# Encoder layer in float32: a second plain half in the up projection, h's sums behind the first one, T4 of w_down's first chunk summed in DRAM, and two quarters of hT changing places

## The chip, the cores and the metric

The kernel runs on one core of a Trainium2 chip. The metric is the device time of one execution in microseconds. Engines are named as in the profile: PE multiplies matrices (PEld loads its weights), DVE and ACT work on vectors, POOL issues the transfers that add or that go from DRAM to DRAM, SP issues most of the plain loads and stores.

## The reference

One layer of an encoder over 512 tokens of 2048 channels, all in float32. Only its second half is touched by the change:

```
x  = x + rms_norm(concat(a, p) @ w_o)                     # a: attention, p: pooling
h  = rms_norm(x)                                          # (512, 2048)
up = causal_dwconv(h @ w_up)                              # w_up (2048, 11264), 3 taps along the tokens
y  = (gelu(up[..., :5632]) * up[..., 5632:]) @ w_down     # w_down (5632, 2048)
x  = x + rms_norm(y)
```

## The kernel before

**Numbers.** Every float32 operand of a product is split in two: `split` (L136) rounds it on ACT (L140, the high part) and takes the rest on DVE (L141, the low part). A product is then made of two or three passes of PE: high by high, high by low, low by high.

**Products of seven.** Large products are cut in 2 x 2 x 2 blocks, and seven products of sums of blocks are made where a plain multiplication has eight. The sums are numbered 1 to 7. Their names in the profile are the banks that hold them: `qa` (products 1, 6, 7, 4, one upon the other), `qg` (5, then 3) and `qd` (2).

**The up projection** has 44 halves: for each u of 22, one half of gates and one of the factors that they multiply, each 256 channels wide, over 512 tokens and a contraction of 2048. Before the change the first half is plain: 16 blocks of the contraction by 2 by 3 passes, 96 matmuls of 512 columns, named `up` in the profile (`mm3`, L162, L164, L165). Its weights come as four quarters `w_0` to `w_3`. The other 43 halves (k from 0 to 42) are made by seven products, each of 8 wide matmuls (512 columns, L170) and 8 narrow ones (256 columns, L176). The product of each (k, i) stands in `Factors.order`, which `seven` follows: product i of half k has the due number 7k plus its place, so that the products of neighbouring halves alternate. The products (0..3, 1) and (0..3, 2), which need only the first 256 tokens of h, are put ahead, then come four entries `("w", q)` for the plain half, then (0,5) and (0,3), and from there (0,6), (0,7), (1,5), (0,4), (1,3), (1,6), (1,7), (2,5), (1,4), (2,3), (2,6), (2,7), and so on.

**The left side** is h turned (tokens along the free axis): `hT`, four tiles of 16 KB per partition, two for each half of the contraction, each holding both halves of the tokens in high and low parts. The last 256 tokens are turned by `turn` (PE, line 1012) among the last early products and in the first two quarters of the plain half, then split into hT. Products 5, 6 and 3 need sums of the blocks of h: `h_sums` (L1374) makes them with 8 additions on DVE, and splits their results into the tiles `h5`, `h6`, `h3`. It also overwrites two quarters of hT (its first contraction half, last tokens) with the difference that product 7 needs, which must wait until the plain half has read them.

**The weights of the seven products** are sums too, and are made in place: a tile is loaded (SP), split, then the next block is added onto it by an accumulating DMA (POOL, L1108), split again. So product 6's weights follow product 5's by one such round, 4 follows 6, and 7 follows 3. `Factors.prefetch` keeps the splits four products ahead of PE. After a bank is done, ACT copies it out (`m`, L1415, L1420, L1424) before the next product may go upon it; each pair of halves ends in a gate (three taps, gelu) or a product with a gate on ACT and DVE, and is stored to DRAM (`gd`, L1346).

**Who sets the order.** PE's instructions run as written. For the other engines a scheduler orders the instructions when the program is built; each engine then runs its own in that order, so one that waits holds up those behind it.

**The down projection** runs over five chunks of w_down, by seven products for each of two column blocks cc, 24 matmuls each (banks `pa`, `pg`, `pd`). The sums of the first chunk are made ahead of time, T5, T7 and T6 in DRAM by `sums_in_dram` (its steps are taken one by one by `more_sums`, in the attention's and the output projection's time), three of the products ready split (`rw`, loaded by POOL at L1212). T4 is T6 loaded, with one more block added onto it in SBUF by an accumulating DMA when it is there (L1241). The tiles of this stage (pool `p4`) lie where hT and the weights of the up projection lay: the four buffers of `part` (copies of product banks) in the quarter at the lowest address, the fifth `part` and the first `bh` (`wh`, first filled with `rw02h`) in the next one. Before the change the lowest quarter holds hT[1] and the next one hT[2]. Products 7 read hT[0] and hT[1]; products 2 and 4 read hT[2] and hT[3], and the last products of the up projection are 7, 2 and 4 of its last half, in this order.

## Time and profile before

| | |
|---|---|
| median of 3 runs | 1881.85 us (1880.81 to 1882.25) |
| the profiled execution | 1881.14 us, its span 1879.3 us |
| PE busy | 1846.3 us, 98% of the span |
| DVE, ACT, POOL busy | 1488.1, 1104.6, 310.4 us |
| DMA | 428.11 MB; 37.7% (SP's queue) and 47.3% (POOL's queue) of the 16 engines' span |
| first plain half on PE | 573.4 to 599.2 us |
| seven products of the up projection, from there | 599.2 to 1434.2 us |
| first chunk of the down projection | 1434.2 to about 1510 us |

Times in the rows are microseconds from the span's start. A row of the timeline gives start, duration, engine, line, operation, tile written and tiles read, and in brackets how long the engine sat idle before it and who released it. A row of the waits gives the instruction that waited, whom for, the sum, how often, and the longest. A row of the windows gives a stretch, its length, each engine's busy time with its instructions, then PE's granted clock (1.00 is full), the DMA engines' busy share and GB/s.

### The profile page before, as it was taken

The page shows a single profiled execution, that of the slowest core. Times are in us where ns is not written, and L with a number is a line of the kernel's source. Part 1 is how long each engine was busy: PE and PEld are TensorE (multiplying, and loading weights), DVE is VectorE, ACT ScalarE, POOL GpSimd, SP SyncE. Part 2 cuts the span into 40 slices and gives each one's busy share as a digit, 9 for nine tenths or more (in the row PEclk, how much of TensorE's full clock was granted, in tenths as well). Part 3 has the DMA queues.
Part 4 walks back from the last instruction along what each step waited for, and adds up shares of the span by engine and source line. Part 5 has one row for each costly group of instructions (what it writes and reads, how often), then busy time and mean ns, then how long its engine had stood idle before and what let it go on. Part 6 is the DMA issues. An engine that isn't in the chain of part 4 may idle for free.

```text
span 1879.3 us, 25378 instructions
## 1 busy us (share of the span) xinstructions
PE 1846.3 (98%) x9530; PEld 1582.3 (84%) x9530; DVE 1488.1 (79%) x1782; ACT 1104.6 (59%) x1449; POOL 310.4 (17%) x411
## 2 busy tenths in 40 slices
PE   9999999999998899999999999999999989999998
PEld 7888888888886788888888888888887878888886
DVE  6988778788678678777787777877776699899876
ACT  7655455466586556665666656666564565565553
POOL 3411001100001221212222121221221101111101
PEclk9999999999999999999999999999999999999999
DMA  8699987999976888888889889888887967877785
GB/s 317 180 315 298 322 233 220 279 279 304 343 261 184 189 187 199 208 207 199 199 202 209 206 196 205 200 204 205 200 179 286 331 239 174 213 202 174 177 240 148
DMA packets 139402, 428.11 MB, mean 228 GB/s; under 512 B 12016, under 2 KB 15472, under 8 KB 133616
## 3 DMA queue, kind: packets, MB, share of 16 engines
q0 software_dynamic: 56016, 177.75, 47.3%
q1 hardware_dynamic: 83264, 248.74, 37.7%
q8 instruction: 75, 1.23, 0.3%
q14 instruction: 47, 0.39, 0.1%
HBM read 372.45 MB, written 100.14 MB: 251 GB/s over the span
## 4 chain that ended last, share of the span: by engine, by line
PE 62%; DMA 3%; DVE 3%; issue 2%; ACT 1%; POOL 0%; POOLq 0%; DVEq 0%; ACTq 0%; SPq 0%
PE qa L170 16%; PE qa L176 8%; PE qg L170 8%; PE qg L176 4%; PE qd L170 4%; PE pa L162 3%; PE pa L164 3%; PE pa L165 3%; PE qd L176 2%; PE pg L162 2%; PE pg L164 2%; PE pg L165 2%; DMA t<-in_w_down 1%; PE pd L164 1%; PE pd L165 1%
## 5 line engine op out<-in xcount | busy, mean ns | idle before, releaser
L170 PE MATMUL qa<-gT,wfh 128*128 128x512 f32 x1200 | 302.0, 394 | 0.0
L141 DVE TENSOR_TENSOR wfl<-x,wfh 128x1024 fp32r<-128x1024 f32 x165 | 202.0, 1224 | 89.4 <-ACT wfh L140 83.5
L170 PEld LDWEIGHTS qa<-gT,wfh 128*128 128x128 f32 x1200 | 216.9, 190 | 38.9
L140 ACT ACTIVATE wfh<-x 128x1024 fp32r<-128x1024 f32 x165 | 174.4, 1057 | 94.7 <-PE qg L170 48.6
L1108 POOL DMA_DIRECT2D x<-in_w_up x125 | 107.2, 858 | 494.0 <-DVE wfl L141 458.6
L170 PE MATMUL qg<-h,wfh 128*128 128x512 f32 x688 | 172.2, 392 | 7.9 <-DVE h L141 6.9
L176 PE MATMUL qa<-gT,wfl 128*128 128x256 f32 x1200 | 169.1, 284 | 5.6 <-ACT m L1420 5.6
L176 PEld LDWEIGHTS qa<-gT,wfl 128*128 128x128 f32 x1200 | 158.6, 192 | 11.1 <-ACT m L1420 6.8
L170 PEld LDWEIGHTS qg<-h,wfh 128*128 128x128 f32 x688 | 129.8, 189 | 36.3 <-DVE h L141 7.5
L140 ACT ACTIVATE bh<-b 128x2048 fp32r<-128x2048 f32 x56 | 106.1, 1914 | 69.8 <-DVE b L1222 26.8
L140 ACT ACTIVATE wfh<-wy 128x1024 fp32r<-128x1024 f32 x100 | 105.3, 1054 | 69.2 <-PE qd L170 50.9
L141 DVE TENSOR_TENSOR bl<-b,bh 128x2048 fp32r<-128x2048 f32 x56 | 127.0, 2285 | 18.8 <-ACT bh L140 11.7
L141 DVE TENSOR_TENSOR wfl<-wy,wfh 128x1024 fp32r<-128x1024 f32 x100 | 121.8, 1218 | 12.7 <-ACT wfh L140 9.6
L162 PE MATMUL pa<-bh,ah 128*128 128x512 f32 x320 | 125.7, 393 | 4.8 <-ACT part L1271 4.8
L164 PE MATMUL pa<-bl,ah 128*128 128x512 f32 x320 | 125.5, 392 | 0.0
L165 PE MATMUL pa<-bh,al 128*128 128x512 f32 x320 | 125.2, 391 | 0.0
L176 PEld LDWEIGHTS qg<-h,wfl 128*128 128x128 f32 x688 | 93.9, 190 | 6.8
L170 PE MATMUL qd<-gT,wfh 128*128 128x512 f32 x400 | 99.0, 390 | 0.0
L176 PE MATMUL qg<-h,wfl 128*128 128x256 f32 x688 | 96.0, 282 | 0.0
L170 PEld LDWEIGHTS qd<-gT,wfh 128*128 128x128 f32 x400 | 74.8, 188 | 15.3
L170 PE MATMUL qa<-h,wfh 128*128 128x512 f32 x344 | 86.2, 392 | 0.0
L141 DVE TENSOR_TENSOR wfl<-wz,wfh 128x1024 fp32r<-128x1024 f32 x50 | 61.2, 1224 | 30.9 <-PE qa L170 28.1
(569 smaller groups left out, 4266.8 us busy)
## 6 DMA issues: line engine op xcount, KB each, us to landing
x<-in_w_up POOLq DMA_DIRECT2D x125, 512.0 KB, 6.1
b<-in_w_down SPq DMA_DIRECT2D x32, 1024.0 KB, 6.9
wt<-in_w_o POOLq DMA_DIRECT2D x24, 1024.0 KB, 15.7
wz<-in_w_up SPq DMA_DIRECT2D x43, 512.0 KB, 5.6
x<-in_w_up SPq DMA_DIRECT2D x43, 512.0 KB, 5.1
wy<-in_w_up SPq DMA_DIRECT2D x43, 512.0 KB, 4.1
wy<-in_w_up POOLq DMA_DIRECT2D x43, 512.0 KB, 6.3
sum<-part POOLq DMA_DIRECT2D x38, 512.0 KB, 7.5
```

The lines of the kernel that those rows point to most:

```text
L140: rounded = nc.scalar.activation(hi, src, AF.Copy)
L141: rest = nc.vector.tensor_sub(lo, src, f32(hi))
L162: nc.tensor.matmul(ps, l[0], r[0], start=first, stop=False, skip_group_check=onto)
L164: nc.tensor.matmul(low, l[0], r[1], start=False, stop=False, skip_group_check=onto)
L165: nc.tensor.matmul(ps, l[1], r[0], start=False, stop=last, skip_group_check=onto)
L170: nc.tensor.matmul(ps, w[0][:, kb], pairs[kb][0], start=fresh and not kb, stop=last, skip_group_check=not fresh)
L176: nc.tensor.matmul(ps[:, sl], w[1][:, kb], pair[:, sl], start=False, stop=last, skip_group_check=not fresh)
L1108: nc.gpsimd.dma_start(self.raw[k, what], self.block(k, m, kh), accum_op=ALU.add)
```

## The change

The second half (the one that u = 0's gate is multiplied with) becomes plain too: `PLAIN` is 2, and the seven products make 42 halves where they made 43. The plain halves are now made by `plain(p, behind)`: behind the quarters of the first one the last tokens are turned, as before; `h_sums` is called after it; behind the quarters of the second one run the four steps of `sums_in_dram` that now make T4 (two copies of T6, two additions), and, after the first two, the splits that overwrite hT's quarters. The gate of u = 0 and its product follow the halves that they belong to. `first_right` loads T4 like any other sum, and its accumulating DMA is gone. hT[1] and hT[2] exchange their buffers, so that hT[2] now lies in the lowest quarter and hT[1] in the one that the fifth `part` and the first `bh` take later.

```diff
--- before.py
+++ after.py
@@ -28,7 +28,7 @@
 EPS = 1e-6
 WARM = 9
 NU = KF // 2
-PLAIN = 1
+PLAIN = 2
 CU = 4
 AHEAD = 3
 SCALE = 1.0 / math.sqrt(DH)
@@ -293,7 +293,7 @@
 
 
 
-    first_sum = {i: [dram.tile([P, CU, S], F32, name=f"t{i}{cc}") for cc in range(2)] for i in (5, 7, 6)}
+    first_sum = {i: [dram.tile([P, CU, S], F32, name=f"t{i}{cc}") for cc in range(2)] for i in (5, 7, 6, 4)}
 
     def sums_in_dram():
 
@@ -327,7 +327,7 @@
                             (copy, 7, (1, 1)), (add, 7, (0, 1)), (copy, 4, 6), (add, 4, (1, 0))):
             yield from wo_step(step, i, at)
         for step, i, at in ((copy, 5, (0, 0)), (add, 5, (0, 1)), (copy, 7, (1, 1)), (copy, 6, 5),
-                            (add, 7, (0, 1)), (add, 6, (1, 1))):
+                            (add, 7, (0, 1)), (add, 6, (1, 1)), (copy, 4, 6), (add, 4, (1, 0))):
             for cc in range(2):
                 step(first_sum[i][cc], first_block(cc, *at) if type(at) is tuple else first_sum[at][cc])
                 yield
@@ -1029,6 +1029,7 @@
         for t in range(2):
             load_x(t, acc8(f"x{t}", "B"))
         hT = new_gT()
+        hT[1], hT[2] = hT[2], hT[1]
         x2(0, y11, 0, whole)
         x2(0, y12, 1, whole)
         keep_x(0)
@@ -1077,7 +1078,7 @@
                        (n - 1, 7), (n - 1, 2), (n - 1, 4)]
                 order = sorted((7 * k + at, k, i) for k in range(n) for i, at in place_of.items())
                 self.order = begin + [(k, i) for _, k, i in order if (k, i) not in begin + end] + end
-                self.order[8:8] = [("w", q) for q in range(4)]
+                self.order[8:8] = [("w", q) for q in range(4 * PLAIN)]
                 self.raw, self.made, self.loaded, self.used = {}, [], 0, 0
 
             def block(self, k, m, kh):
@@ -1234,11 +1235,9 @@
     def first_right(cc, i, ring):
 
         v = ring(f"t{i}")
-        source = first_sum[6 if i == 4 else i][cc] if i in (4, *first_sum) else first_block(cc, *{2: (1, 0), 3: (1, 1)}[i])
+        source = first_sum[i][cc] if i in first_sum else first_block(cc, *{2: (1, 0), 3: (1, 1)}[i])
         with tc.issue_after(first_right.last) if first_right.last else nullcontext():
             first_right.last = nc.sync.dma_start(v, source).ins
-        if i == 4:
-            nc.gpsimd.dma_start(v, first_block(cc, 1, 0), accum_op=ALU.add)
         return v
 
     first_right.last = first_right.part = None
@@ -1386,9 +1385,8 @@
             for a11, a21, a12, a22 in halves:
                 nc.vector.scalar_tensor_tensor(a12, a22, -1.0, a12, op0=ALU.mult, op1=ALU.subtract)
             for i in range(2):
-                split(*quarter(0, 1, i), halves[i][1])
-            for i in range(2):
                 keep(3, i, (3, 2)[i], halves[i][2])
+            return [v[1] for v in halves]
 
         banks, gates = {}, {}
 
@@ -1471,20 +1469,34 @@
         start(3, 2)
         turn(2, 3)
         factors.open = True
-        ups = [bank(f"up0_{j}") for j in range(2)]
-        for q in range(4):
-            factors.used += 1
-            factors.prefetch(0)
-            factors.prefetch((2, 2, 3, factors.AHEAD)[q])
-            w = weights.get(f"w00_{q}", 0)
-            for kb in range(4 * q, 4 * q + 4):
-                for j in range(2):
-                    mm3(ups[j], part(w, j, slice(kb % 4 * P, (kb % 4 + 1) * P)), g_both(hT, kb),
-                        kb == 0, kb == KD - 1)
+        def plain(p, behind):
+            ups = [bank(f"up{p}_{j}") for j in range(2)]
+            for q in range(4):
+                factors.used += 1
+                factors.prefetch(0)
+                factors.prefetch(factors.AHEAD if p else (2, 2, 3, factors.AHEAD)[q])
+                w = weights.get(f"w{p}0_{q}", 0)
+                for kb in range(4 * q, 4 * q + 4):
+                    for j in range(2):
+                        mm3(ups[j], part(w, j, slice(kb % 4 * P, (kb % 4 + 1) * P)), g_both(hT, kb),
+                            kb == 0, kb == KD - 1)
+                behind(q)
+            return ups
+
+        def turn_two(q):
             if q < 2:
                 turn(4 + 2 * q, 5 + 2 * q)
-        h_sums()
+
+        def keep_a21(q):
+            more_sums(1)
+            if q < 2:
+                split(*quarter(0, 1, q), a21_11[q])
+
+        ups = plain(0, turn_two)
+        a21_11 = h_sums()
         gates[0] = gate(0, plain_z(ups))
+        ups = plain(1, keep_a21)
+        product(0, gates.pop(0), plain_z(ups))
         rights, firsts = [right(0, cc) for cc in range(2)], []
         for r in rights:
             next(r)
@@ -1494,7 +1506,7 @@
             r = rights[cc].send(i)
             firsts.append((firsts[0][0] if firsts else first_left(), r))
 
-        for k, i in factors.order[12:]:
+        for k, i in factors.order[8 + 4 * PLAIN:]:
             seven(k, i)
             keep(k, i)
             if (k, i) == (end, 6):
```

How the change moves instructions is shown at three places, in rows of the built programs. The first is DVE at the end of h's sums. In these rows `h` are the tiles that the products 5, 6 and 3 read, `a` the blocks of h that are summed, `wfl` the low part of weights of the seven products, `w_3l` that of a plain half's last quarter, `zc` the taps of the gate. Before, from the last third of the sums on:

```order
L141 TENSOR_TENSOR h_5661<-a_5255,h_5661 128x4x256
L141 TENSOR_TENSOR wfl<-wy,wfh 128x1024
L1384 SCALAR_TENSOR_TENSOR a_5255<-a_5255,a_4847 128x1024
L141 TENSOR_TENSOR gT_4821<-a_5254,gT_4821 128x4x256
L1387 SCALAR_TENSOR_TENSOR a_5001<-a_5255,a_5001 128x1024
L141 TENSOR_TENSOR h_5666<-a_5255,h_5666 128x4x256
L1311 SCALAR_TENSOR_TENSOR zc<-zc,vec 128x511
L141 TENSOR_TENSOR h_5678<-a_5001,h_5678 128x4x256
L141 TENSOR_TENSOR h_5675<-a_5001,h_5675 128x4x256
L1312 SCALAR_TENSOR_TENSOR zc<-zc,vec 128x510
L1311 SCALAR_TENSOR_TENSOR zc<-zc,vec 128x511
L141 TENSOR_TENSOR wfl<-x_5493,wfh 128x1024
```

And in the changed kernel:

```order
L141 TENSOR_TENSOR w_3l<-w_3r,w_3h 128x1024
L1386 SCALAR_TENSOR_TENSOR a_5003<-a_5257,a_5003 128x1024
L141 TENSOR_TENSOR h_5669<-a_5257,h_5669 128x4x256
L1310 SCALAR_TENSOR_TENSOR zc<-zc,vec 128x511 x2
L141 TENSOR_TENSOR h_5674<-a_5003,h_5674 128x4x256
L1311 SCALAR_TENSOR_TENSOR zc<-zc,vec 128x510 x2
L141 TENSOR_TENSOR wfl<-wx,wfh 128x1024
L141 TENSOR_TENSOR gT_4822<-a_5256,gT_4822 128x4x256
L141 TENSOR_TENSOR wfl<-wy,wfh 128x1024
L141 TENSOR_TENSOR gT_4824<-a_5256,gT_4824 128x4x256
L141 TENSOR_TENSOR h_5677<-a_5003,h_5677 128x4x256
```

Before, PE's product (0,5) stands directly behind the plain half, and the last h tile, which product (0,3) needs, stands behind a split of weights, two additions, a hT split and a tap. Now the weights between the sums are those of the second plain half, the last sums are followed by two hT splits that stand behind its first two quarters, and the 96 matmuls of the second plain half stand between the first one and (0,5).

The second place is SP's queue after the last quarter of the first plain half's weights (`w_3r`). `x`, `wy`, `wz` are weights of the seven products, `t` the sums of w_down in DRAM. Before:

```order
L152 DMA w_3r<-in_w_up 128x2x512
L1088 DMA x_5493<-in_w_up 128x1024
L1088 DMA wy<-in_w_up 128x1024 x2
L1088 DMA x_5493<-in_w_up 128x1024
L1088 DMA wy<-in_w_up 128x1024 x2
L1088 DMA wz<-in_w_up 128x1024
L1088 DMA x_5783<-in_w_up 128x1024 x2
L1088 DMA wy<-in_w_up 128x1024
L1088 DMA wz<-in_w_up 128x1024
```

And in the changed kernel:

```order
L152 DMA w_3r<-in_w_up 128x2x512
L1089 DMA x_5619<-in_w_up 128x1024
L152 DMA w_0r<-in_w_up 128x2x512
L152 DMA w_1r<-in_w_up 128x2x512
L1089 DMA x_5619<-in_w_up 128x1024
L152 DMA w_2r<-in_w_up 128x2x512
L152 DMA w_3r<-in_w_up 128x2x512
L312 DMA t_114<-t_112 16x16384
L312 DMA t_115<-t_113 16x16384
L1089 DMA wy<-in_w_up 128x1024 x4
L1089 DMA x_5923<-in_w_up 128x1024 x2
L1089 DMA wz<-in_w_up 128x1024
L1089 DMA wy<-in_w_up 128x1024
```

The second half's four quarters now stand where the first `wy` loads stood, and the two copies T6 to T4 stand ahead of the `wy` loads. On POOL the two additions that finish T4 stand behind the first two additions onto `x`, ahead of the first one onto `wx`:

```order
L1109 DMA x_5619<-in_w_up 128x1024 x2
L316 DMA t_114<-in_w_down 512x1x512
L316 DMA t_115<-in_w_down 512x1x512
L1109 DMA wx<-in_w_up 128x1024
L1109 DMA wy<-in_w_up 128x1024
L1109 DMA wx<-in_w_up 128x1024
L1109 DMA x_5923<-in_w_up 128x1024
L1109 DMA x_5619<-in_w_up 128x1024
L1345 DMA gd_0_5258<-zc 128x2x256
```

The third place is POOL in the first chunk of the down projection. Before, `rw` being the ready products, `sum` the stores of results, `t` the additions that made T4:

```order
L1212 DMA bh<-rw02h 128x2048
L1212 DMA bl<-rw02l 128x2048
L1596 DMA gd_5267<-ca 128x1024
L1300 DMA sum_5268<-part 128x2x512 x2
L1241 DMA t_13315<-in_w_down 128x4x512
L1241 DMA t_13353<-in_w_down 128x4x512
L1300 DMA sum_5269<-part 128x2x512 x2
L1300 DMA sum_5271<-part 128x2x512 x2
```

And in the changed kernel:

```order
L1213 DMA bh<-rw02h 128x2048
L1213 DMA bl<-rw02l 128x2048
L1608 DMA gd_5269<-ca 128x1024
L1299 DMA sum_5270<-part 128x2x512 x2
L1299 DMA sum_5271<-part 128x2x512 x2
L1299 DMA sum_5273<-part 128x2x512 x2
```

The two additions onto `t` between the stores of sums are gone; the rest keeps its order.

## The prediction

> **What bounds the kernel now.** I read first the page's busy times, then PE's waits, then the timeline around each wait, then the windows between them.
>
> ```profile
> PE 1846.3 (98%) x9530; PEld 1582.3 (84%) x9530; DVE 1488.1 (79%) x1782; ACT 1104.6 (59%) x1449; POOL 310.4 (17%) x411
> 657.16:1434.18 777.02, 777.02 (x4465) 686.30 (x4464) 603.26 (x759) 471.93 (x617) 166.05 (x200) 1.00 0.87 200
> ```
>
> PE is the bound. The second row is the long stretch of seven products: busy for all of its 777.02 us at full clock. 4464 matmuls are 279 products of 16, so a product costs 2.785 us and a half of seven 19.5 us. Nothing on another engine can shorten that stretch. What can be won lies in the waits outside it:
>
> ```profile
> PE qg L170 <- DVE h L141: 6.9, 2, 6.5
> PE qa L176 <- ACT m L1420: 5.6, 3, 4.2
> PE pa L162 <- ACT part L1271: 4.8, 1, 4.8
> PE pd L164 <- DMA bl<-rw02l: 2.4, 1, 2.4
> PE up L164 <- DVE gT L141: 1.6, 1, 1.6
> PE qg L170 <- ACT m L1415: 1.0, 1, 1.0
> ```
>
> The first, second and last row belong to the start of the seven products (599 to 657 us), the third and fourth to the first chunk of the down projection. Each long wait costs more than its length, because the clock falls to half and comes back late:
>
> ```profile
> 606.00:607.00 1.00, 0.00 (x0) 0.00 (x0) 1.00 (x3) 1.00 (x2) 0.00 (x0) 0.50 0.00 0
> 609.26 3.56 PE L170 MATMUL qg<-h,wfh 128*128 128x512 f32 x8 [6.47 <-DVE h L141]
> 613.62 1.12 PE L176 MATMUL qa<-h,wfl 128*128 128x256 f32 x8
> 652.17 2.07 PE L176 MATMUL qa<-gT,wfl 128*128 128x256 f32 x8 [4.18 <-ACT m L1420]
> 657.16 2.01 PE L170 MATMUL qg<-h,wfh 128*128 128x512 f32 x8
> 1448.06 0.50 PE L164 MATMUL pd<-bl,ah 128*128 128x512 f32 x1 [2.37 <-DMA bl<-rw02l]
> 1452.27 0.39 PE L162 MATMUL pd<-bh,ah 128*128 128x512 f32 x1
> 1508.94 0.80 PE L162 MATMUL pa<-bh,ah 128*128 128x512 f32 x1 [4.78 <-ACT part L1271]
> 1513.69 0.39 PE L165 MATMUL pa<-bh,al 128*128 128x512 f32 x1
> ```
>
> The granted clock stands seventh in a window's row (0.50 in the first). The product begun at 609.26 ends at 613.62, 4.36 us instead of 2.785: 1.6 lost. The one begun at 652.17 takes 4.99: 2.2 lost. From 1448.06 to 1452.27 there are 11 matmuls, from 1508.94 to 1513.69 another 11; 11 at full clock take 2.5 (0.227 each, by the starts of the many in a row in this stage), so 1.7 and 2.25 are lost.
>
> **The change part by part. (a) A plain half for one of seven.**
>
> ```profile
> 587.89 0.47 PE L162 MATMUL up<-gT,w_2h 128*128 128x512 f32 x1
> 593.46 0.39 PE L162 MATMUL up<-gT,w_3h 128*128 128x512 f32 x1
> 599.18 1.07 PE L170 MATMUL qg<-h,wfh 128*128 128x512 f32 x4
> ```
>
> Two quarters of the first plain half without turning behind them take 5.57 and 5.72 us, 24 matmuls each; four take 22.6. It replaces 19.5: **+3.1 us**, between 2.8 and 3.4 by the one quarter or the other. This is paid on PE in any case.
>
> **(b) h's sums behind the first half.**
>
> ```profile
> 585.62 1.22 DVE L1381 TENSOR_TENSOR a<-a,a 128x1024 f32<-128x1024 f32 x1
> 574.25 3.39 SPq L1088 DMA_DIRECT2D wy<-in_w_up  x2
> 606.20 0.74 DVE L1311 SCALAR_TENSOR_TENSOR zc<-zc,vec 128x511 f32<-128x511 f32 x1
> 606.86 2.35 DVE L141 TENSOR_TENSOR h<-a,h 128x1024 fp32r<-128x1024 f32 x2
> ```
>
> The sums begin at 585.62 and end with the two h splits at 609.2. In the changed kernel DVE has 22 instructions of this size from the first sum to the last h split, splits of weights and hT among them, and 4 taps: 22 x 1.17 + 4 x 0.74 = 28.7, from 585.62 to about 614. PE now makes 96 more matmuls from 599.2 to 621.8, (0,5) follows, and (0,3), which needs the last h, comes at 624.6: 10 us to spare. The second half's own weights ride on the same queues: SP's order puts their loads where four `wy` loads stood, the last of them issued by 577.6 (574.25 + 3.39), and their splits follow the first half's quarters, each some 15 us ahead of use. So the wait of 6.9 and the 1.6 of slow clock go: **-8.4 us** (0.40 + 6.47 + 1.57). If the cover failed altogether, 0.
>
> **(c) The start of the seven products.** The rest of the waits there are 5.6 + 1.0 and 2.2 of clock, 8.7 us. They are not h's:
>
> ```profile
> 634.95 0.86 POOL L1108 DMA_DIRECT2D wy<-in_w_up  x1 [4.76 <-DVE wfl L141]
> 640.53 1.06 ACT L140 ACTIVATE wfh<-wy 128x1024 fp32r<-128x1024 f32 x1 [3.42 <-DMA wy<-in_w_up]
> 651.54 0.58 ACT L1420 ACTIVATE m<-qa 128x512 f32<-128x512 f32 x1
> 613.44 0.86 POOL L1108 DMA_DIRECT2D x<-in_w_up  x1 [0.38 <-ACT zc L1333]
> ```
>
> For the halves 1 and 2, whose products 1 and 2 were made ahead, product 7's split stands two products (5.6 us) after product 3's, but the round between them (DVE, POOL's issue at 634.95, landing at 640.5) is longer. ACT stands at that split, and the copies that PE waits for stand behind it: PE was done at 647.99, the copy began at 651.54. The changed order keeps these rounds and moves a gate from half 1 to half 0, ahead of (1,6)'s copy; so the pattern stays, a half earlier. What gets lighter: the addition at 613.44, half 3's, falls into the second plain half and no longer stands ahead of (1,7)'s round. I take 6.0 for 8.7: **-2.7 us**, nearest to the rows; the bounds are all gone (-8.7), and as much worse as I hope for better (+2.7).
>
> **(d) hT[1] and hT[2].**
>
> ```profile
> 1433.73 0.54 POOL L1212 DMA_DIRECT2D bh<-rw02h  x1 [9.01 <-PE qa L170]
> 1434.25 0.55 POOL L1212 DMA_DIRECT2D bl<-rw02l  x1
> 1428.61 1.98 PE L170 MATMUL qd<-gT,wfh 128*128 128x512 f32 x8
> 1445.04 1.06 ACT L1271 ACTIVATE part<-pa 128x512 f32<-128x512 f32 x2
> 1455.47 1.22 DVE L141 TENSOR_TENSOR al<-s,ah 128x1024 fp32r<-128x1024 f32 x1
> ```
>
> POOL waits for the last reader of the buffer under `bh`, which is hT[2], read by the last product 4. Afterwards it is hT[1], last read by product 7, which ends where `qd` begins, 1428.61: 5 us earlier. `rw02l` landed 13.8 us after its issue; 5 earlier is 1443.0, and PE wants it at 1445.7. What comes free later, the buffers of `part`, is first written at 1445.04. So 2.37 and 1.7 go. Next in line is product (0,5), then due two products of 24 matmuls after 1445.2, at 1456.1; its left side (`al<-s`) was ready at 1456.7, and I leave 0.4: **-3.7 us**. Bounds -4.1 and 0 (if the queue brings it no sooner).
>
> The Trainium skill, TensorE: Matmul & The Clock Gate, "Part 1: The HAM clock gate", says that the clock falls to half after at least one idle window of about 3.4 us. By it the wait of 2.37 us would have cost no clock and (d) would be -2.0. The trace disagrees, since 11 matmuls after it took 4.21 us; the measurement decides.
>
> **(e) T4.**
>
> ```profile
> 1481.42 1.29 POOL L1241 DMA_DIRECT2D t<-in_w_down  x1 [1.35 <-DMA t<-t]
> 1505.54 1.91 ACT L140 ACTIVATE bh<-t 128x2048 fp32r<-128x2048 f32 x1 [8.09 <-DMA t<-in_w_down]
> 1485.07 0.51 SPq L1536 DMA_DIRECT2D gc<-gd  x1
> 1503.98 1.22 DVE L1548 TENSOR_TENSOR s<-gc 128x1024 f32<-128x1024 f32 x1 [3.60 <-DMA gc<-gd]
> ```
>
> The second addition onto T4 is issued at 1481.42 and lands at 1505.5, 24 us later. ACT stands at its split, and the copy of `part` that frees PE's bank stands behind. The changed kernel loads the finished T4, there when the addition was only issued. The `gc` load issued at 1485.07, which the same copy stands behind, took until 1504 in competition with the additions; without them I expect it some 8 us earlier, before the bank is due at about 1500. So 4.78 and 2.25 go: **-7.0 us**, at worst 0.
>
> T4's four transfers (two copies, two additions) move into the plain halves, 578 to about 612 us. That is the copies' 16.6 and the additions' 17.3 (rows below), side by side. Cover: the plain half needs none of them, and the first addition behind them has until 627.
>
> **Sum**, against the profiled execution's 1881.14: +3.1 - 8.4 - 2.7 - 3.7 - 7.0 = -18.7, 1862.4. It lies 0.7 below the median of the runs, so the forecast is **1863 us**. The wait of 1.6 for gT stays.
>
> **The rivals.**
>
> ```profile
> t<-in_w_down POOLq DMA_DIRECT2D x12, 1024.0 KB, 17.3
> wt<-wt POOLq DMA_DIRECT2D x8, 1024.0 KB, 16.6
> wx<-in_w_up POOLq DMA_DIRECT2D x3, 512.0 KB, 5.9
> ```
>
> *T4's additions hold up the weights (slower).* They stand ahead of the first `wx` addition in POOL's queue, without which (0,6), due at 599.2 + 22.6 + 2 x 2.785 = 627.4, has no weights. The copies, issued at 578, land 16.6 later, 594.6. If two additions at the worst row's 24.0 follow each other, they end at 642.6, `wx` lands at 648.5, its splits take 2.3: PE waits 23.4, loses 2.2 of clock and 3.1 more for `wy` behind it. That is 1863 + 28.7 = 1892. It decides from an end of the additions at 636 (21 us each in a row). Against it: at the median of 17.3 they end at 629 even in a row, and the one issued at 1481.42 ran beside another. By the Trainium skill (DMA: Bandwidth & Descriptors, "Queues, rings and completion order") each DMA engine takes turns between the queues but consumes one queue's descriptors in order; no run here shows this apart, and by it only POOL's own additions would be held, as assumed.
>
> *The wait at 1504 stays, with another name.* `gc` lands at 1504 as before, for it is queued behind two loads of `b` in a full DMA: the 7.0 stays, 1870. For it: it landed 19 us after its issue. Against: two accumulating megabytes are gone from that stretch.
>
> *h is late again.* ACT or DVE stands at a split of the second half's weights, and the last h comes after 624.6; some 8 us stay, 1871. Against: 10 us to spare.
>
> *The start runs clean.* With 22 us more for DMA all the 8.7 of (c) go: 1857. Against: the rounds for halves 1 and 2 begin only with their product 3, after the plain halves.
>
> *It does not do what it says*: waits move and PE merely pays the plain half, 1881 to 1884.
>
> **How the numbers follow.** Forecast (1859 to 1867) 0.57; clean start 0.10; wait at 1504 stays 0.14; h late again 0.07; no gain 0.06 (0.05 of it within 0.2%, 0.01 slower); T4's additions 0.06, of which 0.05 beyond 0.2% slower and 0.01 short of it, still faster. About 0.2%, 3.8 us, is what a measurement of this kernel tells from no change. Faster: 0.57 + 0.10 + 0.14 + 0.07 + 0.01 = 0.89; same 0.05; slower 0.06. The range goes from the clean start with (d) whole, 1856, to the wait at 1504 kept and (c) at its worse bound, 1873.
>
> **What would show it.** Right: no wait of PE on h; 96 matmuls of `up` more in 22 to 23 us; no PE wait on `rw02l` and `bh<-rw02h` issued right after product 7; no addition onto `t` near 1480 and no wait of PE on `part`; waits on `m` of about 6 us with their clock. Wrong: a wait on `wfl` at the first (0,6) would show T4 in the way; a wait on `part` released by ACT behind `gc`, the second rival; slow clock after short waits, more loss than I count.

## The result, and the profile after

The changed kernel takes 1862.2 us (median of 4 runs, 1860.06 to 1864.22) against 1881.99 (4 runs) on the same chip: a ratio of 0.9896, 95% interval 0.9879 to 0.9913. The forecast was 1863, range 1856 to 1873. The profiled execution took 1864.22, its span is 1862.4; that of before has 1879.3, so the two traces differ by 16.9 us. The sum in the prediction had said 18.7. The total is right; of its five terms, (d) did not come at all and (a) lies outside its bounds. That the forecast comes within 0.8 us of the median is in part luck: the profiled execution, in which the terms are measured below, lies 2.0 us above it.

First the page's busy times of the changed kernel:

```profile
PE 1843.5 (99%) x9514; PEld 1580.2 (85%) x9514; DVE 1482.2 (80%) x1772; ACT 1101.1 (59%) x1442; POOL 306.9 (16%) x407
```

and PE's waits (us in total, times, longest):

```profile
PE qa L176 <- ACT m L1418: 3.4, 3, 2.0
PE qg L170 <- ACT m L1413: 1.9, 3, 0.9
...
PE pd L164 <- DMA bl<-rw02l: 1.5, 1, 1.5
...
PE pd L162 <- ACT ah L140: 0.9, 1, 0.9
```

The wait on `h` (6.9) and the one on `part` (4.8) are gone. Those on `m` went from 6.6 to 5.3. The one on `rw02l` did not go: 1.5 is left of 2.4, and 0.9 on `ah` has joined it.

To see where each microsecond went, I cut the run at three instructions of PE that both kernels have: the first matmul of `up`, the first of product (0,5), the first of `pa`. The windows of before, then those of after (start and end, length, busy time of PE, PEld, DVE, ACT and POOL, PE's granted clock, DMA share, GB/s):

```profile
573.37:599.18 25.81, 24.24 (x115) 19.68 (x113) 20.98 (x20) 15.78 (x24) 3.45 (x4) 1.00 0.77 174
599.18:1434.18 835.00, 821.53 (x4689) 723.14 (x4688) 642.83 (x804) 505.07 (x660) 175.45 (x211) 0.99 0.86 198
1434.18:1870.90 436.72, 429.56 (x1885) 354.53 (x1883) 362.19 (x269) 239.61 (x251) 50.64 (x50) 0.99 0.80 221
```

```profile
572.66:619.96 47.30, 45.72 (x212) 37.78 (x210) 36.91 (x35) 28.79 (x38) 5.93 (x7) 1.00 0.93 246
619.96:1424.99 805.03, 799.74 (x4577) 704.32 (x4576) 620.40 (x778) 487.37 (x639) 172.05 (x207) 1.00 0.87 200
1424.99:1854.20 429.21, 426.81 (x1885) 353.01 (x1883) 362.29 (x269) 240.22 (x251) 47.93 (x48) 1.00 0.78 220
```

The plain halves grew by 21.49, the seven products shrank by 29.97 (19.5 of it is the half that is no longer made of seven), the down projection by 7.51. What lies before the first `up`, where the program is the same, was 0.71 shorter (in the other profiles it begins between 572.5 and 574.3, in one, plain3's, at 578.0), the tail 0.2. Together 16.9.

### The profile page after: what moved, and what is told of

It is laid out like the page before. It is cut to its first block, busy times and chain, and to the rows that moved or that the text cites. A ratio compares the mean times of both kernels' runs of the same rounds, so it can differ in the third digit from the quotient of the medians.

```text
span 1862.4 us, 25317 instructions
## 1 busy us (share of the span) xinstructions
PE 1843.5 (99%) x9514; PEld 1580.2 (85%) x9514; DVE 1482.2 (80%) x1772; ACT 1101.1 (59%) x1442; POOL 306.9 (16%) x407
## 4 chain that ended last, share of the span: by engine, by line
PE 66%; DMA 1%; DVE 1%; ACT 1%; issue 0%; POOL 0%; DVEq 0%; POOLq 0%; ACTq 0%
PE qa L170 16%; PE qa L176 8%; PE qg L170 8%; PE qg L176 4%; PE pa L165 4%; PE pa L162 4%; PE pa L164 4%; PE qd L170 4%; PE pg L165 2%; PE pg L162 2%; PE pg L164 2%; PE qd L176 2%; PE pd L164 1%; PE pd L165 1%; PE pd L162 1%; PE up L164 1%
## 5 line engine op out<-in xcount | busy, mean ns | idle before, releaser
L170 PE MATMUL qa<-gT,wfh 128*128 128x512 f32 x1176 | 295.9, 394 | 0.0
L141 DVE TENSOR_TENSOR wfl<-x,wfh 128x1024 fp32r<-128x1024 f32 x161 | 197.1, 1224 | 83.0 <-ACT wfh L140 76.8
L170 PEld LDWEIGHTS qa<-gT,wfh 128*128 128x128 f32 x1176 | 212.5, 190 | 38.2
L140 ACT ACTIVATE wfh<-x 128x1024 fp32r<-128x1024 f32 x161 | 170.1, 1056 | 88.9 <-PE qg L170 47.3
L176 PE MATMUL qa<-gT,wfl 128*128 128x256 f32 x1176 | 165.1, 283 | 3.4 <-ACT m L1418 3.4
L170 PE MATMUL qg<-h,wfh 128*128 128x512 f32 x672 | 166.4, 390 | 1.9 <-ACT m L1413 1.9
L170 PEld LDWEIGHTS qg<-h,wfh 128*128 128x128 f32 x672 | 125.8, 188 | 28.9 <-ACT m L1413 2.9
L141 DVE TENSOR_TENSOR wfl<-wy,wfh 128x1024 fp32r<-128x1024 f32 x98 | 119.4, 1218 | 16.9 <-ACT wfh L140 14.6
```

The source lines that it names most:

```text
L140: rounded = nc.scalar.activation(hi, src, AF.Copy)
L141: rest = nc.vector.tensor_sub(lo, src, f32(hi))
L170: nc.tensor.matmul(ps, w[0][:, kb], pairs[kb][0], start=fresh and not kb, stop=last, skip_group_check=not fresh)
L176: nc.tensor.matmul(ps[:, sl], w[1][:, kb], pair[:, sl], start=False, stop=last, skip_group_check=not fresh)
```

## The experiments

The medians of before on the chips of the four groups below lie between 1882.1 and 1884.4. A few us between two medians are therefore not told apart; ratios to before on the same chip, and the lengths of the three stretches in the profiles, carry the argument.

**The exchange of hT[1] and hT[2] undone (no_swap).**

```diff
-        hT[1], hT[2] = hT[2], hT[1]
```

> The changed kernel without the line that exchanges hT[1] and hT[2]. Theory A: the exchange did nothing, since the quarters' places in SBUF went along with their roles: in both kernels the quarter that product 4 reads last lies at 39936 bytes, under the buffer that rw02h is loaded into (44032), and POOL issued that load 0.45 us before the last product's end in both (1433.73 against 1434.18, 1424.54 against 1424.99). Then this kernel takes the time of the changed one, 1862.2 within 1.5, with the same two waits of PE at the second product of the down projection (0.9 and 1.5 us). Theory B: the exchange did its 3.7 us and something else gave them back; then 1866, with a wait on rw02l of 2.4 us or more.

1864.1 us, 0.9898 [0.9884, 0.9911]: the time of the changed kernel, with the same two waits at the second product, 0.92 and here 1.35 us. Theory A holds. The addresses in the built programs say why (bytes within a partition; the `bh` of rw02h lies at 44032 in all three):

```
role     before           changed          changed, without the exchange
hT[0]    gT0 at 56320     gT0 at 56320     gT0 at 56320
hT[1]    gT1 at 23552     gT2 at 23552     gT1 at 23552
hT[2]    gT2 at 39936     gT1 at 39936     gT2 at 39936
hT[3]    gT3 at 72704     gT3 at 72704     gT3 at 72704
```

The tiles changed roles, and their places changed with them. With addresses put in for names, the built programs of no_swap and of the changed kernel are the same, instruction for instruction. So hT[1] still lies in the lowest quarter after the change, and hT[2] in the one that `bh` takes, not the other way round as the section on the change has it. The changed kernel's timeline shows it at POOL's issue:

```profile
1419.42 1.98 PE L170 MATMUL qd<-gT,wfh 128*128 128x512 f32 x8
...
1424.54 0.53 POOL L1213 DMA_DIRECT2D bh<-rw02h  x1 [9.02 <-PE qa L170]
1424.99 0.39 PE L162 MATMUL pa<-bh,ah 128*128 128x512 f32 x1
...
1436.95 0.49 PE L162 MATMUL pd<-bh,ah 128*128 128x512 f32 x1 [0.92 <-ACT ah L140]
...
1438.92 0.50 PE L164 MATMUL pd<-bl,ah 128*128 128x512 f32 x1 [1.48 <-DMA bl<-rw02l]
```

`bh<-rw02h` is issued 0.45 us before `pa` begins, as it was before the change (1433.73 against 1434.18), not at `qd`, 5 us earlier.

**The exchange done in another way (wh_first).** The ring of right sides takes the place under hT[1], so the buffer comes free after product 7.

```diff
-        for r in (product_part, later["wh"], half_g, later["raw1"], ...
+        for r in (later["wh"], product_part, half_g, later["raw1"], ...
```

> The changed kernel with two rings of the last pool placed the other way round: the right sides' buffers first (23552 to 39936, under the hT quarter that product 7 reads last), the buffers of part behind them. Theory A: this is what the exchange of hT was forecast to do. POOL issues bh<-rw02h about 5.1 us earlier, just before product 7's end, rw02l lands some 5 us earlier than PE wants it, its wait of 1.48 us goes and the clock after it stays up; the wait of 0.92 on ah<-gc stays: 1.5 + 1.7 = 3.2 us less, 1859. Theory B: the landing of rw02l is set by the two transfers ahead of it and gc on the DMA engines, not by its issue: it lands no sooner, 1862. Theory C: the earlier 2 MB hold up gc, which is issued at the same moment, and PE waits for ah<-gc longer than 0.92: 1861 to 1863.

1864.47 us, 0.9902 [0.9887, 0.9916]: nothing won, though the issue moved as wanted. Its timeline:

```profile
1423.10 0.54 POOL L1213 DMA_DIRECT2D bh<-rw02h  x1 [4.36 <-PE qa L170]
...
1428.20 0.39 PE L162 MATMUL pa<-bh,ah 128*128 128x512 f32 x1
...
1441.94 0.50 PE L164 MATMUL pd<-bl,ah 128*128 128x512 f32 x1 [1.28 <-DMA bl<-rw02l]
```

and the window ahead of the landing, columns as above:

```profile
1434.00:1442.00 8.00, 5.80 (x26) 4.25 (x24) 1.22 (x1) 2.95 (x4) 0.00 (x0) 1.00 1.04 420
```

The load is issued 5.10 us before `pa`, 4.65 earlier than in the changed kernel. PE gets its data 13.74 us after the start of `pa`, where it had been 13.93: 0.2 us for 4.65. The window's row has the likely reason in its last two columns, a DMA share of 1.04 at 420 GB/s. So theory B, as far as the time goes; which transfers stood ahead is not shown. Theory C's hold-up doesn't show: the two `gc` loads of this stretch land 16.9 us after their issue (median) against 16.7 in the changed kernel.

**Two right sides made ahead instead of three (ready2).** (0,2) is then read as 1 MB raw, no longer as 2 MB ready.

```diff
-    READY = (0, 1), (1, 1), (0, 2)
+    READY = (0, 1), (1, 1)
```

> The changed kernel with two right sides of the down projection made ahead instead of three: (0,2) is no longer read as two ready parts of 1 MB each (rw02h, rw02l) but as its raw 1 MB, which ACT and DVE split then. From 1419 to 1439 us the DMA engines' busy share is 1.04 to 1.06 at 395 to 419 GB/s, and issuing rw02h and rw02l 4.7 us earlier moved the end of the wait by 0.2 us only. Theory A: what is late at the second product is set by the bytes ahead of it in that stretch, not by the issue or the buffer. One MB less is 2.5 us at 419 GB/s, ACT and DVE stand idle there (7.6 to 8.8 us) and can split: the wait of 1.48 on rw02l goes with its 1.7 us of clock, and the 0.92 on gc at least in part: 1858 to 1859. Theory B: the split, 1.9 on ACT and 2.3 on DVE, stands in the raw load's way instead, and PE waits on it about as long: 1861 to 1863.

1862.37 us, 0.9889 [0.9876, 0.9903]; not told from the changed kernel by time. The timeline tells more:

```profile
1427.38 1.92 ACT L140 ACTIVATE bh<-t 128x2048 fp32r<-128x2048 f32 x1 [2.23 <-DMA t<-in_w_down]
...
1435.05 0.50 PE L162 MATMUL pd<-bh,ah 128*128 128x512 f32 x1 [0.92 <-ACT ah L140]
...
1436.30 0.50 PE L165 MATMUL pd<-bh,al 128*128 128x512 f32 x1 [0.53 <-DVE al L141]
```

The wait on the right side is gone, its high part split by 1429.3, and the clock stays at 1.00. That agrees with theory A, but the run does not tell fewer bytes from an earlier place: the raw load is issued at 1412.1, before the DMA engines are full. The 0.92 on `ah` stays to the hundredth, which theory A had not expected, and 0.53 on `al`, made by DVE right behind `ah`, is late next. From `pa` to the end it takes 427.36 us against 429.21, as much as no_swap, where the clock happened to stay up behind both waits (427.46).

**The left sides' rings exchanged (ah_moved).** The 0.92 had the same length in ten profiles of this program and its relatives, and the releaser that ACT's row names is PE, not the load of `gc`. The built programs agree: the new `ah` lies at 109568, and since the second plain half so does `a`'s high part, which both of the first two products read. Before the change `a` lay at 121856. This kernel is ready2 and:

```diff
-        for r in (..., later["wl"], slot_h, slot_l, scratch):
+        for r in (..., later["wl"], slot_l, slot_h, scratch):
```

> As ready2, with the rings of the left sides' high and low parts exchanged in the last pool. In the changed kernel and in ready2 the wait of 0.92 on ah<-gc has been the same to the hundredth in every profile, and ACT's idle time before it ends with PE pa, not with gc: the new ah of (0,2) lies at 109568, where the high part a of the first left side lies, and PE reads that until the second product's end. Before the change a lay at 121856 and ah<-gc waited for gc alone. Theory A: this overlap makes the wait, not gc. With ah at 142336 it goes, and the low part, now at 109568, takes 0.5 to 0.7 in its place: 0.8 us less in the down projection than ready2 (426.5 from the first pa to the end, 427.36 there). Theory B: gc lands no sooner, as I had taken it before, and the wait of 0.9 on ah stays.

1862.93 us, 0.9890 [0.9873, 0.9908]: by time no difference again. By the trace it is theory A. The split's row in the changed kernel, then those of this one with PE's next wait:

```profile
1435.84 1.06 ACT L140 ACTIVATE ah<-gc 128x1024 fp32r<-128x1024 f32 x1 [8.77 <-PE pa L164]
```

```profile
1432.36 1.06 ACT L140 ACTIVATE ah<-gc 128x1024 fp32r<-128x1024 f32 x1 [0.49 <-DMA gc<-gd]
...
1436.40 1.22 DVE L141 TENSOR_TENSOR al<-gc,ah 128x1024 fp32r<-128x1024 f32 x1 [2.21 <-PE pa L164]
...
1437.68 0.50 PE L165 MATMUL pd<-bh,al 128*128 128x512 f32 x1 [0.69 <-DVE al L141]
```

ACT splits as soon as `gc` lands, and the wait on `ah` is gone. The low part, now at that address, waits for PE in its place, and PE 0.69 us for it. From `pa` to the end: 426.52, where 426.5 was expected. So the 0.92 is a wait that the second plain half brought: it moved the weights' ring on, and with it the place of `a`.

**T4 as it was (no_t4).**

```diff
+        if i == 4:
+            nc.gpsimd.dma_start(v, first_block(cc, 1, 0), accum_op=ALU.add)
...
-                            (add, 7, (0, 1)), (add, 6, (1, 1)), (copy, 4, 6), (add, 4, (1, 0))):
+                            (add, 7, (0, 1)), (add, 6, (1, 1))):
```

> The changed kernel with T4 as it was before: loaded from the finished T6 and the last block added onto it in SBUF, no sum of T4 in DRAM. Theory A: the four steps of T4 in DRAM cost nothing where they run and are worth the wait on part and its clock: 7.0 us back, 1869.2, with a PE wait of 4 to 5 us on part some 70 us into the down projection. Theory B: T4's transfers beside the plain halves cost something there, as the waits of 0.8 to 2.1 us on m: then those get shorter too, and the time is 1866 to 1868.

1873.64 us, 0.9950 [0.9936, 0.9963]; that is 9.5 more than no_swap on the same chip. The profiled execution took 1871.17, 7.0 more than the changed kernel's; it is the fastest of five. That is theory A, at 7.0 by the profile and 9.5 by the medians. In the profile all of it is in the down projection, which is as long as before the change. The start is no lighter without T4's transfers: `up` begins 1.12 us later than in the changed kernel, and the first addition onto `wx` is issued 1.11 us later, at 609.93. The windows of the seven products and of what follows:

```profile
621.08:1424.40 803.32, 798.10 (x4578) 703.08 (x4576) 620.11 (x778) 487.36 (x639) 171.60 (x207) 1.00 0.88 200
1424.40:1861.04 436.64, 427.74 (x1885) 352.86 (x1883) 362.18 (x269) 239.48 (x251) 50.57 (x50) 1.00 0.79 221
```

and PE's longest wait:

```profile
PE pa L162 <- ACT part L1272: 6.2, 2, 5.1
```

(803.32 is 1.7 under the changed kernel's 805.03. Here the clock stayed up after a wait of 2.06; there it fell. It also stayed up here behind the waits at the second product of the down projection, 0.92 and 1.58, where the changed kernel's fell. So 436.64 is better set against no_swap's 427.46, where the clock stayed up there too: 9.2, close to the 9.5 of the medians. The last section comes back to the clock.)

**T4 alone (t4_only).** The kernel before, with the sum of T4 in DRAM, its four steps behind the quarters of the single plain half. (The lines that add T4 to the sums and take its accumulating DMA away, the same as in the change, are left out here.)

```diff
...
             if q < 2:
                 turn(4 + 2 * q, 5 + 2 * q)
+            more_sums(1)
         h_sums()
```

> The kernel before with the sum of T4 in DRAM alone, its four steps behind the four quarters of the one plain half. Theory A: the sum of T4 is worth the same without the second plain half: the kernel before less 7.0, 1875, with the waits on h (6.9) and m (6.6) as they were; then the second plain half with h's sums is worth the rest, about 10 to 12. Theory B: without the second plain half the two additions of 17 us each stand ahead of the weights of product (0,6) in POOL's queue, PE waits there on wfl or m up to 10 us longer than before, and the time is 1880 or more.

1882.48 us (11 runs), 0.9989 [0.9980, 0.9998]. Alone, the sum of T4 brings next to nothing. It does what it is for. The same two windows of this kernel:

```profile
598.67:1443.12 844.45, 823.17 (x4689) 724.54 (x4688) 647.29 (x807) 507.69 (x662) 176.33 (x212) 0.99 0.87 198
1443.12:1872.37 429.25, 426.78 (x1885) 353.12 (x1883) 362.19 (x269) 240.21 (x251) 47.91 (x48) 1.00 0.79 220
```

and its timeline where the seven products begin:

```profile
581.71 1.17 POOL L316 DMA_DIRECT2D t<-in_w_down  x1 [2.28 <-DMA t<-t]
582.83 0.96 POOL L1108 DMA_DIRECT2D wx<-in_w_up  x1
...
602.19 1.06 ACT L140 ACTIVATE wfh<-wx 128x1024 fp32r<-128x1024 f32 x1 [9.52 <-DMA wx<-in_w_up]
...
609.10 2.08 PE L170 MATMUL qg<-h,wfh 128*128 128x512 f32 x4 [9.36 <-DVE h L141]
```

The down projection is 7.47 shorter than before, and the seven products are 9.45 longer. The addition onto `wx` stands right behind T4's second addition on POOL and lands 19.4 us after its issue; ACT stands 9.52 us at its split, DVE behind ACT, and `h`'s sums behind DVE. PE waits 14.2 us on `h` (9.36 and, at (0,3), 4.83) in place of 6.9. This is the prediction's first rival, with theory B's cause, at another waiter: `h`, not `wfl`. The DMA engines were full in that stretch (a share of 1.06 from 572.85 to 598.67, against 0.77 before the change), so the run doesn't tell whether POOL's order or the mere bytes held the addition up. In the changed kernel T4's additions are issued at 588.88 and 592.35 and the next `wx` addition only at 608.82, 16 us behind them.

With before, no_t4 and the changed kernel this makes a square. Lengths of the two stretches, from the profiles (us; 19.5 taken off the first where there is one plain half, as it holds one half of seven more):

```
                      T4 in SBUF                T4 in DRAM
one plain half        815.5 + 436.7 (before)    825.0 + 429.3 (t4_only)
two plain halves      803.3 + 436.6 (no_t4)     805.0 + 429.2 (changed)
```

T4 in DRAM wins 7.4 in the down projection either way as the profiles stand, and 9.2 under two halves where the clock is alike (no_t4). It costs 9.5 at the start under one plain half. Under two it costs nothing: the 1.7 between 803.3 and 805.0 is the fall of the clock.

**h's sums written behind the second half (h_late).**

```diff
...
         ups = plain(0, turn_two)
-        a21_11 = h_sums()
         gates[0] = gate(0, plain_z(ups))
-        ups = plain(1, keep_a21)
+        ups = plain(1, lambda q: more_sums(1))
+        a21_11 = h_sums()
+        for q in range(2):
+            split(*quarter(0, 1, q), a21_11[q])
```

> The changed kernel with two plain halves, but h's sums written behind the second half instead of the first. Theory A: the whole gain of the second plain half is the cover for h's sums; without it the wait for h of 6.5 to 6.9 us with 1.6 us of clock comes back, 8.4 in all: 1870.6. Theory B: DVE is less loaded behind the second half (four of its weight splits are gone), so a part of the cover stays: 1866 to 1868.

1863.15 us, 0.9898 [0.9882, 0.9914]: no change, and no wait on `h`. Both theories fall, on a premise they share: that the place in the text sets the place on DVE. It does not here. The first sum begins at 584.9 in both, and the last split of `h` is this, in the changed kernel and in h_late:

```profile
614.29 1.23 DVE L141 TENSOR_TENSOR h<-a,h 128x1024 fp32r<-128x1024 f32 x1 [1.13 <-ACT h L140]
```

```profile
613.70 1.22 DVE L141 TENSOR_TENSOR h<-a,h 128x1024 fp32r<-128x1024 f32 x1 [1.13 <-ACT h L140]
```

The scheduler put the sums in nearly the same places though their text stood behind the second half; by which rule, the run doesn't show. What the change gave `h` is PE's 96 matmuls, not a place: (0,5) begins at 619.96, 4.4 us after the last split, where before the change it began 10 us ahead of it (599.18 and 609.2).

**A third plain half (plain3).**

```diff
-PLAIN = 2
+PLAIN = 3
...
         product(0, gates.pop(0), plain_z(ups))
+        gates[1] = gate(1, plain_z(plain(2, lambda q: None)))
```

> The changed kernel with a third plain half, the first half of the next block, behind the second. Theory A: a plain half costs 21.8 against 19.5, 2.3 us, and the halves' gates fall again as in the kernel before, where waits on m with their clock took 8.7 us against 6.8 in the changed kernel: 1862.2 + 2.3 + 1.9 = 1866.4. Theory B: which half has the gate makes no difference to the waits: 1864.5. Theory C: another 22 us of plain matmuls give the additions onto the weights time, so the waits on m shrink: 1862 or less.

The third half reads two quarters of hT that hold a sum by then, so it makes the same instructions on other numbers: only its time is of use, its result is not the layer's. 1872.5 us, 0.9938 [0.9924, 0.9952]. The profiled execution, the slowest of five, began `up` 5.4 us later than the changed kernel's, by short waits between 7 and 482 us that have nothing to do with the halves; beyond that, its first two windows:

```profile
578.03:647.08 69.05, 67.48 (x307) 55.81 (x306) 45.97 (x45) 35.47 (x46) 8.26 (x9) 1.00 0.82 219
647.08:1435.40 788.32, 781.29 (x4465) 688.16 (x4464) 604.32 (x758) 476.40 (x624) 166.08 (x200) 1.00 0.87 198
```

The half costs 21.75 (69.05 less 47.30), 2.25 more than seven products. The seven products are 2.8 longer than the changed kernel's less 19.5, with a wait on `m` of 3.48 at full cost in clock. That fits theory A, 4.2 forecast and 5.0 found in these two stretches; theory C falls. By the ratios the kernel is some 8 us slower than the changed one, twice theory A's figure, and what lies beyond the 5.0 I don't place.

**Product 3 sooner (three_sooner).**

```diff
-                order = sorted((7 * k + at, k, i) for ...
+                order = sorted((7 * k + (4.5 if i == 3 and k in (1, 2) else at), k, i) for ...
```

> The changed kernel with product 3 of the halves 1 and 2 one product earlier (ahead of product 4 of the half before), so that the addition onto wy has 2.8 us more before product 7's split wants it. Theory A: ACT's standing at that split (4.14 us before 638.13) is what holds up the copies of m: the wait of 0.87 goes and that of 2.05 shrinks, with 1.7 us of clock: 2 to 4 us less, 1858 to 1860. Theory B: the wait of 2.05 is ACT's own work by then (busy from 643.5 to 647.6 without a break), so only 0.9 goes or other copies of m come late instead: 1861 to 1863.

1872.64 us, 0.9941 [0.9928, 0.9953], by the ratios some 9 us slower than the changed kernel, which neither theory had. The addition onto `wy` is in time now; the split at 635.56 no longer waits for it. From the timeline:

```profile
635.56 1.06 ACT L140 ACTIVATE wfh<-wy 128x1024 fp32r<-128x1024 f32 x1 [1.26 <-PE qg L170]
...
639.15 0.81 ACT L1310 ACTIVATE zc<-zc,vec 128x512 f32<-128x512 f32 x1 [2.53 <-DMA gd<-zc]
...
640.50 3.06 PE L170 MATMUL qg<-h,wfh 128*128 128x512 f32 x8 [4.07 <-ACT m L1414]
...
684.86 1.52 ACT L1310 ACTIVATE zc<-zc,vec 128x512 f32<-128x512 f32 x2 [6.08 <-DMA gd<-zc]
...
690.77 2.08 PE L176 MATMUL qa<-gT,wfl 128*128 128x256 f32 x8 [3.78 <-ACT m L1419]
```

But the next gate comes ahead of the copies of `m` on ACT, and its first instruction waits until the store of the gate before (`gd<-zc`) has read their common buffer: 2.53 and 6.08 us. PE waits 4.07 and 3.78 for the copies behind. In these rows ACT works in order: whichever of its instructions waits for a DMA holds up the copies behind it.

**The gelu behind the copy (gelu_behind), and both (best).** These ran with the changed kernel itself (after_again).

```diff
...
-            nc.scalar.activation(flat(a), flat(a), AF.Gelu_apprx_tanh)
+            with tc.issue_after(behind) if behind else nullcontext():
+                nc.scalar.activation(flat(a), flat(a), AF.Gelu_apprx_tanh)
...
```

(`behind` is the copy of product 6 of the next half, for the gates of k below 4; best also has ready2's line.)

> The changed kernel once more, on the chip of the next two. 1862 to 1864. Of its two short waits (2.05 at the start of the seven products, 0.9 with 1.5 at the down projection's second product) each costs 1.5 to 1.8 us of clock in some executions and nothing in others (3 of 6 and 3 of 6 profiles so far), so single runs should lie within about 4 us of each other.

> The changed kernel with one exchange on ACT in each of the first gates: the gelu of gate 1 (1.04 us from 646.07) behind the copy of (1,6), which stood behind it and for which PE waited 2.05 us until 647.65. Theory A: ACT's order at that point is what the rest of (c) is made of: the copy runs 1.0 us sooner, the wait shrinks to about 1.1, too short to cost clock: 1.0 us plus the 1.7 of clock where it was lost, 1860 to 1862. Theory B: the copy is held by something else (DVE's part of the gate, the split of wy at 645.13), the wait stays 2 us and the time is that of the changed kernel.

> Both together: the gelu behind the copy, and two right sides made ahead instead of three. Theory A: each takes away one of the two waits after which the clock can fall, 1.0 and 1.0 us of idle time and up to 1.7 of clock each: 1858 to 1861, and single runs closer together than those of the changed kernel. Theory B: single runs differ for other reasons, the spread stays and the median is within 1 us of the changed kernel's.

The changed kernel takes 1864.53, 0.9893 [0.9879, 0.9908]; gelu_behind 1863.75, 0.9893 [0.9877, 0.9909]; best 1862.95, 0.9886 [0.9869, 0.9903]. None is told from another, and single runs of best spread as much (1860.8 to 1866.5) as those of the rest, so theory B for it: no version here beats the changed kernel by more than its measurement is uncertain. In gelu_behind the wait did shrink, and another came (timeline):

```profile
647.49 1.21 PE L176 MATMUL qa<-gT,wfl 128*128 128x256 f32 x8 [1.42 <-ACT m L1419]
...
655.84 1.06 ACT L140 ACTIVATE wfh<-wy 128x1024 fp32r<-128x1024 f32 x1 [4.66 <-DMA wy<-in_w_up]
...
657.43 2.11 PE L170 MATMUL qg<-h,wfh 128*128 128x512 f32 x8 [1.32 <-ACT m L1414]
```

2.05 became 1.42 where 1.1 was expected, and the next addition onto `wy`, which the changed kernel's PE reaches 1.8 us later after its wait and slow clock (657.71 less 619.96, against 656.11 less 620.20), is now 1.32 us late. Here the next wait took what was taken from the one before.

## Why the prediction was right, step by step

**(a), mis-sized.** The term said +3.1; it is +2.0 (21.49 less 19.5), below the lower bound of 2.8. The two quarters that I took "without turning behind them" belong to the first half, and each has something that the second half hasn't. In the one of 5.57 us the last turning, issued at 587.09 for 1.04 us, reaches into the quarter's start. In the one of 5.72, PE's weight load waits for the last tokens' split. The row of before, and a window of the changed kernel over 24 matmuls of the second half:

```profile
593.84 0.19 PEld L164 LDWEIGHTS up<-gT,w_3h 128*128 128x128 f32 x1 [0.41 <-DVE gT L141]
```

```profile
602.28:607.72 5.44, 5.44 (x26) 4.50 (x24) 5.44 (x8) 3.22 (x4) 0.00 (x0) 1.00 0.84 207
```

24 at the 0.227 us that the prediction itself had for the down projection are 5.45, and four of them 21.8: the row for it was at hand. The second half takes 21.76 (598.20 to 619.96), 2.3 more than seven products. The first half, without that wait, became 0.27 shorter (25.54 for 25.81); the two together are the +2.0.

**(b), right.** No wait on `h`, -8.4. Its reason needs a correction: not that the sums are written behind the first half (h_late), but that PE has 21.8 us of work that needs no `h` while DVE makes it. The last split ends at 615.5, where the step had said 614; (0,3), which needs it, could have begun at 622.88, 7.4 us later (10 forecast).

**(c), right in kind, a little large.** Forecast 6.0 left of 8.7; left are 5.1 of waits and 1.7 of clock (below, the product begun at 647.65 ends at 652.11, 4.46 for 2.785), so -1.9 and not -2.7. Together (b) and (c) are -10.3; the stretch says -10.5. ACT's order is part of the cause, as argued: in the changed kernel the copy stands behind a split and a gelu, and with the gelu behind it the wait is 1.42 (gelu_behind).

```profile
645.13 1.04 ACT L140 ACTIVATE wfh<-wy 128x1024 fp32r<-128x1024 f32 x1
646.07 1.04 ACT L1332 ACTIVATE zc<-zc 128x1024 f32<-128x1024 f32 x1
647.02 0.57 ACT L1418 ACTIVATE m<-qa 128x512 f32<-128x512 f32 x1
647.65 1.57 PE L176 MATMUL qa<-gT,wfl 128*128 128x256 f32 x8 [2.05 <-ACT m L1418]
...
652.11 2.01 PE L170 MATMUL qg<-h,wfh 128*128 128x512 f32 x8
```

But the step's reason, ACT standing at the `wy` split for a late load, is not what these rows show: from 643.46 to the copy ACT waits for nothing. Nor was the `wy` split of 640.53 the one next to the late copy before the change. Nearer to that copy, at 651.54, ACT waited for a transfer into `x`:

```profile
646.72 1.06 ACT L140 ACTIVATE wfh<-x 128x1024 fp32r<-128x1024 f32 x1 [2.72 <-DMA x<-in_w_up]
```

The round that was to get lighter did not: ACT's wait at the `wy` split is 4.14 us before 638.13 in the changed kernel, 3.42 before the change. So the 6.0 that I kept for 8.7 came near 6.8 in part by luck; what shortened the wait from 4.18 to 2.05 no run takes apart.

**(d), the step that failed.** It said: the buffer under `bh` is afterwards hT[1], "last read by product 7 [...]: 5 us earlier", and "`rw02l` landed 13.8 us after its issue; 5 earlier is 1443.0". The first half was wrong because the exchange of names exchanged the addresses too; nothing moved (no_swap). The second half was wrong as well: where the issue did move, by 4.65 us, the data came 0.2 us earlier, in a stretch in which the DMA engines were full (wh_first). The 0.4 us left for the next wait should have been 0.6 by the step's own rows (1456.7 less 1456.1). The bound named for it, 0 "if the queue brings it no sooner", is what came, for both reasons: 0.9 and 1.5 of waits and about 1.7 of clock, against 2.4 and 1.7 before. The 0.9 is a wait that the prediction did not see at all: a tile's address moved on with its ring (ah_moved). That the change does not do what it says was a rival for the whole; it held for this one part, which had no such rival of its own.

**(e), right.** -7.0 forecast; the down projection is 7.5 shorter, with (d) at nothing. The second rival fell: the `gc` load that it is about took 18.9 us before the change (issued at 1485.07, used from 1503.98). In the changed kernel DVE uses it 11.0 us after its issue and waits for nothing, so it came the 8 us sooner that (e) had expected, or more.

```profile
1475.93 0.45 SPq L1548 DMA_DIRECT2D gc<-gd  x1
...
1486.90 1.21 DVE L1560 TENSOR_TENSOR s<-gc 128x1024 f32<-128x1024 f32 x1
```

Its cover, "the plain half needs none of them", was right for two halves only, and the first rival shows the price without it (t4_only). The prediction gave that rival its chance as if it could strike the changed kernel; its condition is met by the same edit one plain half short. By its own medians two additions in a row would have ended at 629, past the 627 that (e) gave them. In the changed kernel they are not in a row: they are issued at 588.88 and 592.35, 3.5 us apart.

So: +2.0 - 8.4 - 1.9 + 0 - 7.5 = -15.8; 0.7 and 0.2 come from the parts that were not touched, and 0.2 I don't place: 16.9. Of the 18.7 forecast, 3.7 from (d) and 0.8 from (c) did not come; 1.1 from (a), 0.5 from (e) and the 1.1 just named made up for more than half of it. The forecast time was met the better for a start that happened to be 0.7 shorter.

## What to carry to other kernels

An edit's price belongs to the arrangement it is put in: T4 in DRAM was worth 7 to 9.5 us with a second plain half as its cover, and 0.1% of the time without, so pieces of one change are to be measured together and apart. Before counting on a buffer that comes free earlier, look at the addresses in the built program, where they can go along with a name or move on with a ring, and at whether the DMA engines are full in that stretch. Where an in-order engine holds the copies that PE waits for, shortening one wait can show the next one, as in gelu_behind and three_sooner.

## What the runs showed of the hardware that I had not expected

**Short waits cost clock by chance.** Over the fourteen profiles, each wait of PE after 570 us falls into one of these, by the granted clock behind it:

- 2.37 us and longer, 13 waits up to 9.36: the clock fell to 0.50 every time.
- 2.05 or 2.06, the same wait in eight profiles: it fell in 5 and stayed in 3.
- 0.92 and then 1.28 to 1.64, with half a us of work between, in eight profiles: it fell in 4, stayed in 4.
- other waits, up to 1.77, among them the one of 1.57 at the first `up` in all fourteen: never.

The same wait, first in the changed kernel from one us after its end, then in h_late from its end on:

```profile
648.65:651.65 3.00, 3.00 (x10) 2.42 (x10) 0.06 (x1) 1.06 (x1) 0.60 (x1) 0.50 0.81 195
```

```profile
647.33:650.33 3.00, 3.00 (x17) 2.66 (x18) 1.07 (x2) 1.32 (x2) 0.85 (x1) 1.00 0.87 224
```

10 matmuls against 17 in 3 us. Where it falls it costs about 1.7 us, and the changed kernel has two such waits: up to 3.4 us between one execution and the next. The changed kernel, no_swap and after_again are one program: the clock fell at its second pair of waits in two of the three profiles and stayed in one. The changed kernel's four runs lie 4.2 apart, and the granted clock of each whole run falls as the time grows: 0.999 at 1860.06, 0.998 at 1861.56, 0.997 at 1862.85 and 1864.22. But this is not all of the spread: four runs of gelu_behind have 0.999 and lie between 1862.0 and 1866.3. What moves those, no run shows. The Trainium skill, TensorE: Matmul & The Clock Gate, "Part 1: The HAM clock gate", has a window of about 3.4 us that runs freely. That agrees with the same wait being struck in some executions and spared in others; that a whole idle window is needed does not agree with 2.05 us.

**A full stretch of DMA.** From 1419 to 1439 us the DMA share is 1.05 at 411 GB/s in the changed kernel. In the same stretch of wh_first (1.04 at 420 GB/s ahead of the landing) an issue 4.65 us earlier brought the data 0.2 us earlier.
